# Operands of the up projection stored tile by tile in runs of 2 KB, and the 1/rms row of the attention output spread by a product with ones

## Chip, cores and metric

One Trainium2 chip, one of its cores. The metric is device time in microseconds (us) of one launch, the median over runs. Engines are called as in the profile: PE (TensorE, with PEld for its weight loads), DVE (VectorE), ACT (ScalarE), POOL (GpSimd) and SP (SyncE, which here only issues transfers).

## The reference, cut to what matters

One layer of a hybrid decoder on 2064 prompt rows (16 meta tokens and 2048) and 32 sample rows (8 sequences of 4), model width 1024, inner width 2816, all in fp32.

```python
q, k, v, u = _project(_rmsnorm(x, norm1), w_in)         # one input projection
att = _head_norm(attention(q, k, v, lam), sub_g)        # differential attention, per-head RMSNorm:
                                                        #   o * rsqrt(mean(o * o) + EPS) * g * (1 - lam_init)
ssm_out = _ssm(u, ...)                                  # state space half
x = x + concat([att, ssm_out]) @ w_out                  # output projection
xn = _rmsnorm(x, norm2)
a, c = xn @ w_gate, xn @ w_up                           # the up projection (gate and up)
x = x + (gelu(causal_conv3(a)) * c) @ w_down
```

The sample rows attend to 2048 cached keys and values each, which are gathered by a page table.

## The kernel before, in words

The 2096 rows are 17 tiles of 128 (the last has 48). Products of full accuracy are made of three products in a reduced fp32 format (`mm3`, lines 80 to 82), whose operands are split into a high and a low part by `split` (line 68 on ACT, line 69 on DVE). A scheduler with pools of buffers sets the order of the instructions on each engine when the kernel is built; code that is written later can so fill in where an earlier part waits.

**Attention and output.** `attend` works head by head, in two halves of the rows. It leaves the head outputs untouched by the norm in the DRAM scratch `OT`, and 1/rms as a row per head in the DRAM scratch `RR` (`attend_rms`, `attend_rms_store`: products SS, the chain rs_v, rs_y, rs_t on DVE and POOL, the transpose tpr, a store). `out_heads` then makes one tile of the output projection: it loads the rows of x (`oxt`), the head outputs into `ot[:, 0]`, and the 1/rms row of each head, spread over the 128 partitions by a broadcast transfer, into `ot[:, 1]` (line 1195). POOL multiplies the two (line 1196), ACT and POOL split the result into `oa` (lines 1198, 1199), and 24 products `po` follow for the two halves of the width, each added to `oxt` by DVE (line 1206). `out_norm` norms the rows (line 166 on ACT, the chain of `rsqrt`, line 171 on DVE), transposes them on PE (`tp`, line 179) and stores them as operands.

Tiles 0 to 5 are filler in the attention stage: their pool `fil` has a single PSUM bank for all their products and transposes, and single buffers. Tiles 6 to 15 come after attention, in double buffers and four PSUM banks, where the norm of a tile stands behind the products of the next. This stretch is called the tail below. Tile 16 comes much later, in the up projection.

**Sample attention.** The cached keys are gathered (`kv`, line 607 on POOL), transposed on PE (`tps`, line 632), split (`kT`) and multiplied with the queries (`Sp`, line 638). It is filler from the tail on, well into the up projection.

**Up projection.** It goes by Strassen's scheme in Winograd's form: the even and odd tiles of a block of rows are two halves, and seven operands are made of their quarters (`keep` in `out_norm`). They lie in the DRAM scratch `XB`, for each of three blocks (tiles 0 to 5, 6 to 11, 12 to 16), for each partition and operand four rows of k with up to 384 columns, 128 for each pair of tiles. `load_tokens` loads an operand in two halves of k and splits each into `xb`. `load_up` loads the weights of a unit (256 columns of gate or up) in two loads `uraw`; a unit has seven products of 12 matmuls each for each of the four k (`product`: 84 matmuls). The pool `fr` has four slots `raw` of 4 KB per partition for weights; in later blocks the first half of an operand uses them too. The other halves use slots of the pool `fz` (`z` and `A`, two each), which also hold the conv's data.

Every DMA issued on SP goes in order through one queue, so a load that waits for its buffer holds those behind it.

Of the kernel before, what the change touches and what calls it, by code (L numbers as in the profile page):

```python
# [10 lines left out]
F32 = mybir.dt.float32  # L11
# [4 lines left out]
ALU = mybir.AluOpType  # L16
# [4 lines left out]
P = 128  # L21
# [8 lines left out]
H = 4  # L30
# [16 lines left out]
BLOCKS = [(0, 6), (6, 12), (12, NT)]  # L47
# [13 lines left out]
class Step:  # L61
# [41 lines left out]
    def constants(self, cp, tp):  # L103
        nc, i = self.nc, self.i
# [3 lines left out]
        nc.vector.tensor_copy(self.identB, self.ident)  # L108
        self.half = cp.tile([P, 16], F32, name="half")
        nc.vector.memset(self.half, -0.5)  # L110
        self.ones = cp.tile([P, 32], F32, name="ones")
        nc.vector.memset(self.ones, 1.0)
        cm = tp.tile([P, P], F32, name="cm")
        nc.sync.dma_start(out=cm, in_=i["c_causal"])
# [19 lines left out]
    def scratch(self, dp):  # L134
        self.KST = dp.tile([H, 2, P, TP], F32, name="KST")
        self.QST = dp.tile([2, H, 2, 64, TP], F32, name="QST")
        self.VST = dp.tile([TP, H * P], F32, name="VST")
        self.VNS = dp.tile([NS * TS, H * P], F32, name="VNS")
        self.UT = dp.tile([512, CH, NU], F32, name="UT")
        self.XNT = dp.tile([6, P, 2, KT, 2 * P], F32, name="XNT")  # L140
        self.OT = dp.tile([H, P, T], F32, name="OT")
        self.RR = dp.tile([H, RRW], F32, name="RR")
        self.TBL = dp.tile([3, G, NST, NJ], F32, name="TBL")
        self.GT = dp.tile([CH, 512, NC], F32, name="GT")
        self.ST = dp.tile([2, 4, P, T], F32, name="ST")
        self.X1 = dp.tile([T, D], F32, name="X1")
        self.XB = dp.tile([len(BLOCKS), P, 7, 4, 3 * P], F32, name="XB")
        self.MT = dp.tile([2, P, 11, T], F32, name="MT")

    def load_x(self, xt, t):  # L150
# [1034 lines left out]
    def out_heads(self, t, wp, pp):  # L1185
        nc, gp = self.nc, self.nc.gpsimd
        n = rows_of(t)
# [3 lines left out]
        ot = wp.tile([P, 2, H, P], F32, name="ot", tag="ot")  # L1191
        nc.sync.dma_start(out=ot[:, 0, :, :n], in_=self.OT[:, :, tk].rearrange("h p t -> p h t"))

        for a, b, f in ((0, NM, 0), (NM, P, P)) if t == 0 else ((0, n, t * P + P - NM),):
            nc.sync.dma_start(out=ot[:, 1, :, a:b], in_=self.RR[:, f : f + b - a].unsqueeze(0).to_broadcast([P, H, b - a]))
        gp.tensor_tensor(out=ot[:, 0, :, :n], in0=ot[:, 0, :, :n], in1=ot[:, 1, :, :n], op=ALU.mult)
        a = wp.tile([P, 2, H, P], F32R, name="oa", tag="oa")
        nc.scalar.activation(a[:, 0, :, :n], ot[:, 0, :, :n], AF.Copy)
        gp.tensor_tensor(out=a[:, 1, :, :n], in0=ot[:, 0, :, :n], in1=a[:, 0, :, :n].bitcast(F32), op=ALU.subtract)
        for hf in range(2):  # L1200
            c = slice(512 * hf, 512 * hf + 512)
# [8 lines left out]
    def out_norm(self, t, xt, wp, pp):  # L1210
        nc, gp = self.nc, self.nc.gpsimd
        n = rows_of(t)
        xs = self.normed(wp, xt, n, self.g2)
        blk = min(t // 6, 2)
        at = (t - BLOCKS[blk][0]) // 2 * P
        last = t == NT - 1
        m = n // 2 if last else P
        if t % 2 == 0:
# [5 lines left out]
                nc.scalar.activation(x[:, b, :, :m], tp[:, :, z * m : z * m + m], AF.Copy)  # L1224

        def keep(op, x, o=1):
            nc.scalar.dma_start(out=self.XB[blk, :, op : op + o, :, at : at + m], in_=x)

        if t % 2 == 0:
            keep(0, ev[:, :, :, :m], 2)  # L1230
# [38 lines left out]
    def load_tokens(self, blk, z):  # L1269

        L = width_of(blk)
        op = self.PLACE[z]
        x = self.fx.tile([P, 2, 4, 3 * P], F32R, name="xb", tag=f"xb{op}")
        for k in (0, 2):
            if blk and k == 0:
                raw = self.fr.tile([P, 4, 256], F32, name="xraw", tag="raw", bufs=4).rearrange("p k f -> p (k f)")
            else:

                tag = "A" if blk or k else "z"
                raw = self.fz.tile([P, 6 * P + 2 * (tag == "A")], F32, name="xraw", tag=tag, bufs=2)  # L1280
            raw = raw[:, : 6 * P].rearrange("p (k c) -> p k c", k=2)
            self.nc.sync.dma_start(out=raw[:, :, :L], in_=self.XB[blk, :, op, k : k + 2, :L])
            self.split(x[:, 0, k : k + 2, :L], x[:, 1, k : k + 2, :L], raw[:, :, :L])
        self.xs[z] = x

    def load_up(self, unit):
# [470 lines left out]
```

## Time and profile before

| | |
|---|---|
| median of 3 runs | 2932.37 us (2930.18 to 2940.95) |
| the profiled execution's own time | 2934.36 us |
| its span, first to last instruction | 2932.2 us |
| mean granted PE clock | 0.974 of full speed |
| busy share of the span | PE 94%, PEld 81%, DVE 76%, ACT 48%, POOL 34% |
| transfers | 526.81 MB, mean 180 GB/s |

Busy time of PE counts the modelled ends of pipelined matmuls; idle time of PE is what is left of a stretch. A wait names the instruction that waited, its engine, and what released it. The share of a DMA queue is the time its packets took, as a part of what 16 engines have in the stretch.

### The profile page before, as it was taken

How to read it: one execution, taken by the hardware profiler on the slowest of the kernel's cores; microseconds unless marked ns; L12 is line 12 of the kernel's file. 1: busy time of each engine (PE TensorE's matmuls, PEld its weight loads, DVE VectorE, ACT ScalarE, POOL GpSimd, SP SyncE). 2: the span in 40 equal slices, each digit the busy share in tenths (PEclk: the TensorE clock that was granted, in tenths of full speed). 3: DMA queues.
4: the chain of work that ended last, by engine and by line, in shares of the span. 5: the costliest groups of instructions: out<-in, count | busy, mean ns of one | idle time of the engine just before them, and what ended most of it. 6: DMA issues, size and time to landing. Idle time of an engine off the chain costs nothing. (4 is left out here: it accounts for less than half of the span.)

```text
span 2932.2 us, 43446 instructions
## 1 busy us (share of the span) xinstructions
PE 2742.1 (94%) x14872; PEld 2360.8 (81%) x14872; DVE 2216.4 (76%) x4308; ACT 1397.6 (48%) x2850; POOL 985.0 (34%) x1383
## 2 busy tenths in 40 slices
PE   6889989989999999787999999999999999999999
PEld 6876667867888777676998899988998998777776
DVE  6738876757778888567898878888788996675565
ACT  4323223545556566335566556665555664222233
POOL 4525542114444566554333422343222442000000
PEclk9999999999999999899999999999999999999999
DMA  7975876976764432487455446464454346775562
GB/s 222 258 190 141 211 219 166 239 217 188 222 190 146 117 114 83 145 265 241 145 173 186 155 146 206 152 196 147 133 167 154 118 129 237 266 239 189 168 219 86
DMA packets 450965, 526.81 MB, mean 180 GB/s; under 512 B 91369, under 2 KB 353401, under 8 KB 449720
## 3 DMA queue, kind: packets, MB, share of 16 engines
q1 hardware_dynamic: 359000, 382.86, 44.1%
q10 hardware_dynamic: 72848, 72.79, 7.5%
q0 software_dynamic: 18896, 68.39, 7.4%
q8 instruction: 117, 1.92, 0.3%
q14 instruction: 104, 0.85, 0.1%
HBM read 387.61 MB, written 135.14 MB: 178 GB/s over the span
## 5 line engine op out<-in xcount | busy, mean ns | idle before, releaser
L80 PE MATMUL g<-xb,uw 128*128 128x384 f32 (+1 forms) x1848 | 596.3, 325 | 9.5 <-ACT uw L68 3.7
L81 PE MATMUL g<-xb,uw 128*128 128x384 f32 (+1 forms) x1848 | 595.6, 323 | 1.6 <-DVE xb L69 1.6
L82 PE MATMUL g<-xb,uw 128*128 128x384 f32 (+1 forms) x1848 | 583.6, 323 | 1.6 <-DVE uw L69 1.6
L80 PEld LDWEIGHTS g<-xb,uw 128*128 128x128 f32 x1848 | 347.6, 188 | 21.8 <-ACT uw L68 5.1
L81 PEld LDWEIGHTS g<-xb,uw 128*128 128x128 f32 x1848 | 348.4, 189 | 9.8 <-issue 2.3
L82 PEld LDWEIGHTS g<-xb,uw 128*128 128x128 f32 x1848 | 345.2, 188 | 9.0 <-DVE uw L69 3.1
L475 ACT ACTIVATE p<-S,nms 128x484 f32<-128x484 f32 (+11 forms) x360 | 209.8, 588 | 158.3 <-DVE nms L474 137.0
L69 DVE TENSOR_TENSOR uw<-uraw,uw 128x512 fp32r<-128x512 f32 x330 | 241.8, 739 | 27.0 <-ACT uw L68 25.1
L68 ACT ACTIVATE uw<-uraw 128x512 fp32r<-128x512 f32 x330 | 200.5, 625 | 115.0 <-PE g L82 72.9
L474 DVE TENSOR_REDUCE nms<-S 128x1 f32<-128x484 f32 (+11 forms) x360 | 191.3, 556 | 41.7 <-PE S L469 26.1
L80 PE MATMUL pq<-dw,da 128*128 128x512 f32 x528 | 208.3, 396 | 13.9 <-DVE dO L1586 7.6
L81 PE MATMUL pq<-dw,da 128*128 128x512 f32 x528 | 208.1, 395 | 0.0
L82 PE MATMUL pq<-dw,da 128*128 128x512 f32 x528 | 200.4, 394 | 2.3 <-DVE da L69 2.3
L95 POOL TENSOR_TENSOR rs_y<-rs_v,half 128x8 f32<-128x8 f32 (+4 forms) x77 | 105.3, 1370 | 244.8 <-DVE rs_v L90 225.5
L80 PE MATMUL pj<-wh,x 128*128 128x512 f32 (+1 forms) x408 | 169.9, 418 | 6.7 <-ACT wh L74 4.3
L81 PE MATMUL pj<-wl,x 128*128 128x512 f32 (+1 forms) x408 | 170.1, 417 | 4.8 <-DVE wl L75 4.8
L68 ACT ACTIVATE da<-dt 128x1024 fp32r<-128x1024 f32 (+1 forms) x68 | 71.0, 1045 | 215.5 <-PE pq L82 142.1
L82 PE MATMUL pj<-wh,x 128*128 128x512 f32 (+1 forms) x408 | 169.6, 416 | 0.0
L468 PE MATMUL S<-kt,qs 128*128 128x484 f32 (+11 forms) x360 | 145.5, 406 | 22.8 <-ACT p L475 14.4
L1308 POOL TENSOR_TENSOR uraw<-uraw 128x512 f32<-128x512 f32 x66 | 106.3, 1610 | 176.2 <-DVE s L1306 127.1
L507 DVE SCALAR_TENSOR_TENSOR p<-p,f 128x412 f32<-128x412 f32 (+13 forms) x164 | 139.5, 863 | 25.1 <-POOL p L505 24.9
L505 POOL TENSOR_TENSOR p<-p,g 128x412 f32<-128x412 f32 (+13 forms) x164 | 156.2, 980 | 3.4
(430 smaller groups left out, 6917.6 us busy)
## 6 DMA issues: line engine op xcount, KB each, us to landing
dt<-MT SPq DMA_DIRECT2D x99, 512.0 KB
uraw<-in_w_gate_dram SPq DMA_DIRECT2D x66, 512.0 KB
uraw<-in_w_up_dram SPq DMA_DIRECT2D x66, 512.0 KB
raw<-in_w_in_dram SPq DMA_DIRECT2D x80, 256.0 KB
MT<-z ACTq DMA_DIRECT2D x44, 384.0 KB
qs<-QST SPq DMA_DIRECT2D x128, 128.0 KB
draw<-in_w_down_dram SPq DMA_DIRECT2D x55, 256.0 KB
dT<-in_w_down_dram SPq DMA_DIRECT2D x55, 256.0 KB
```

The costliest lines, as they stand in the source:

```text
L68: nc.scalar.activation(hi, src, AF.Copy)
L69: nc.vector.tensor_tensor(out=lo, in0=src, in1=hi.bitcast(F32), op=ALU.subtract)
L80: mm(out, lhsT=lh, rhs=rh, start=start, stop=False, skip_group_check=goes_on)
L81: mm(out, lhsT=lh, rhs=rl, start=False, stop=False, skip_group_check=goes_on)
L82: mm(out, lhsT=ll, rhs=rh, start=False, stop=stop, skip_group_check=goes_on)
L95: nc.gpsimd.tensor_tensor(out=y, in0=v, in1=e, op=ALU.pow)
L468: nc.tensor.matmul(dst, lhsT=qs[:, 0, c, qa : qa + M], rhs=kt[c][:, x:y], start=True, stop=False)
L474: nc.vector.tensor_reduce(out=nms[:M, z : z + 1], in_=dst, axis=AX.X, op=ALU.max, negate=True)
L475: nc.scalar.activation(p[:M, Z + x : Z + y], dst, AF.Exp, bias=nms[:M, z : z + 1], accum_out=sms[:M, z : z + 1])
L505: nc.gpsimd.tensor_tensor(out=pw[1][:M, x], in0=pw[1][:M, x], in1=g[:M, z : z + 1].to_broadcast([M, x.stop - x.start]), op=ALU.mult)
L507: nc.vector.scalar_tensor_tensor(out=w[:M, x], in0=w[:M, x], scalar=fs[0][:M, z : z + 1], in1=pw[1][:M, x], op0=ALU.mult, op1=ALU.add)
L1308: gp.tensor_tensor(out=a21, in0=a11, in1=a21, op=ALU.subtract)
```

## The change

Two edits are made together.

The scratch `XB` gets the order block, partition, operand, pair of tiles, k, column, instead of block, partition, operand, k, column of the block. A store of one pair's operand is then one run of 4 x 128 numbers (2 KB) per partition and operand, where it was four runs of 512 B. `load_tokens` loads the first two pairs of tiles of an operand as one run of 4 KB per partition into a slot `raw` of `fr`, in every block, and the third pair (24 columns in the last block) into a slot `A` of `fz`; before, it took two halves of k, in block 0 in slots `z` and `A`. For the last tile each operand is stored by a transfer of its own.

The 1/rms row of each head is loaded into one partition alone. A product on PE of a row of ones with it (fp32, one partition deep, up to 512 columns) spreads it over the partitions in a PSUM bank `rrb`, and the multiplication with the head outputs is done by DVE out of that bank, not by POOL. The constant `ones` grows to 128 columns for it.

```diff
-        self.XB = dp.tile([len(BLOCKS), P, 7, 4, 3 * P], F32, name="XB")
+        self.XB = dp.tile([len(BLOCKS), P, 7, 3, 4, P], F32, name="XB")
...
-            nc.sync.dma_start(out=ot[:, 1, :, a:b], in_=self.RR[:, f : f + b - a].unsqueeze(0).to_broadcast([P, H, b - a]))
-        gp.tensor_tensor(out=ot[:, 0, :, :n], in0=ot[:, 0, :, :n], in1=ot[:, 1, :, :n], op=ALU.mult)
+            nc.sync.dma_start(out=ot[0:1, 1, :, a:b], in_=self.RR[:, f : f + b - a].unsqueeze(0))
+        rr = pp.tile([P, 512], F32, name="rrb", tag="ps").rearrange("p (h c) -> p h c", h=H)
+        nc.tensor.matmul(rr[:, :, :n], lhsT=self.ones[0:1, :], rhs=ot[0:1, 1, :, :n], start=True, stop=True)
+        nc.vector.tensor_tensor(out=ot[:, 0, :, :n], in0=rr[:, :, :n], in1=ot[:, 0, :, :n], op=ALU.mult)
...
-        at = (t - BLOCKS[blk][0]) // 2 * P
+        at = (t - BLOCKS[blk][0]) // 2
...
-            nc.scalar.dma_start(out=self.XB[blk, :, op : op + o, :, at : at + m], in_=x)
+
+            for z in range(o) if last else [slice(0, o)]:
+                to = self.XB[blk, :, op + z, at, :, :m] if last else self.XB[blk, :, op : op + o, at]
+                nc.scalar.dma_start(out=to, in_=x[:, z])
...
-        for k in (0, 2):
-            if blk and k == 0:
-                raw = self.fr.tile([P, 4, 256], F32, name="xraw", tag="raw", bufs=4).rearrange("p k f -> p (k f)")
-            else:
-
-                tag = "A" if blk or k else "z"
-                raw = self.fz.tile([P, 6 * P + 2 * (tag == "A")], F32, name="xraw", tag=tag, bufs=2)
-            raw = raw[:, : 6 * P].rearrange("p (k c) -> p k c", k=2)
-            self.nc.sync.dma_start(out=raw[:, :, :L], in_=self.XB[blk, :, op, k : k + 2, :L])
-            self.split(x[:, 0, k : k + 2, :L], x[:, 1, k : k + 2, :L], raw[:, :, :L])
+
+        raw = self.fr.tile([P, 4, 256], F32, name="xraw", tag="raw", bufs=4).rearrange("p (j h) (l c) -> p j (h l) c", j=2, c=P)
+        self.nc.sync.dma_start(out=raw, in_=self.XB[blk, :, op, 0:2])
+        hi, lo = [x[:, s, :, : 2 * P].rearrange("p k (j c) -> p j k c", c=P) for s in range(2)]
+        self.split(hi, lo, raw)
+
+        raw = self.fz.tile([P, 6 * P + 2], F32, name="xraw", tag="A", bufs=2)[:, : 4 * P].rearrange("p (k c) -> p k c", c=P)
+        n = L - 2 * P
+        self.nc.sync.dma_start(out=raw[:, :, :n], in_=self.XB[blk, :, op, 2, :, :n])
+        self.split(x[:, 0, :, 2 * P : L], x[:, 1, :, 2 * P : L], raw[:, :, :n])
```

The scheduler orders every engine anew from the attention stage's first filler tile on. Three places show it; line numbers past 1194 differ between the two kernels by up to five.

On PE, at the start of the tail (tpr is the transpose of the last 1/rms row, po the output products of tile 6, tps the transposes of gathered keys), the kernel before has:

```order
L552 MATMUL SS_12784<-ones_72,o2_11820 128x1 x8
L564 MATMUL tpr_12804<-ident_63,rs_y_12796 8x128
L80 MATMUL po_13903<-owh_13435,oa_13900 128x512
L81 MATMUL po_13903<-owl_13436,oa_13900 128x512
L82 MATMUL po_13903<-owh_13435,oa_13900 128x512
```

and 25 more products of this kind before the first tps. The changed kernel has there:

```order
L564 MATMUL tpr_12804<-ident_63,rs_y_12796 8x128
L1197 MATMUL rrb_13911<-ot_13908,ones_72 128x512
L632 MATMUL tps_14778<-ident_63,kv_14774 128x128 x2
L80 MATMUL po_13917<-owh_13435,oa_13914 128x512
L81 MATMUL po_13917<-owl_13436,oa_13914 128x512
L80 MATMUL po_13931<-owh_13435,oa_13914 128x512
L81 MATMUL po_13931<-owl_13436,oa_13914 128x512
L1197 MATMUL rrb_13951<-ot_13948,ones_72 128x512
L632 MATMUL tps_14778<-ident_63,kv_14776 128x128 x2
L82 MATMUL po_13917<-owh_13435,oa_13914 128x512
```

The product with ones stands ahead of each tile's output products, and these are cut up by key work. Between tpr and the first product of the up projection PE had 128 tps and 61 Sp; now it has 180 tps, 87 Sp and ten rrb, with the same 240 po and 80 tp.

On POOL, at the same place (ot is multiplied in line 1196, oa is the low part, qbd and kv belong to the gathered keys), the kernel before has:

```order
L1196 TENSOR_TENSOR ot_13896<-ot_13896 128x512
L95 TENSOR_TENSOR rs_y_12796<-rs_v_12795,half_70 128x8
L1199 TENSOR_TENSOR oa_13900<-ot_13896,oa_13900 128x512
L1196 TENSOR_TENSOR ot_13934<-ot_13934 128x512
L618 MEMSET qbd_14731 128x1088
L607 DMA kv_14742<-in_cache_k_dram,idx_14699 128x1024
...
L1199 TENSOR_TENSOR oa_13938<-ot_13934,oa_13938 128x512
L624 COPY qbd_14731<-qhl_14727 64x4x4 x8
L1196 TENSOR_TENSOR ot_14000<-ot_14000 128x512
```

and the changed kernel:

```order
L95 TENSOR_TENSOR rs_y_12796<-rs_v_12795,half_70 128x8
L618 MEMSET qbd_14763 128x1088
L607 DMA kv_14774<-in_cache_k_dram,idx_14731 128x1024
...
L624 COPY qbd_14763<-qhl_14759 64x4x4 x8
L1201 TENSOR_TENSOR oa_13914<-ot_13908,oa_13914 128x512
L1201 TENSOR_TENSOR oa_13954<-ot_13948,oa_13954 128x512
L95 TENSOR_TENSOR rs_y_13990<-rs_v_13989,half_70 128x1
```

The multiplications of tiles 6, 7 and 8 are gone from POOL, and the copies into qbd, which wait for gathered keys, stand ahead of the first low parts.

On SP, at the start of the up projection (oxt is the tail's last load of x), the kernel before has:

```order
L1190 DMA oxt<-X_104 128x1024 x3
L1293 DMA uraw<-in_w_gate_dram 128x4x256 x2
L1293 DMA uraw<-in_w_up_dram 128x4x256 x2
L1282 DMA xraw<-XB 128x768 x5
L1293 DMA uraw<-in_w_gate_dram 128x4x256 x2
L1282 DMA xraw<-XB 128x768 x5
L1293 DMA uraw<-in_w_up_dram 128x4x256 x2
```

and the changed kernel:

```order
L1190 DMA oxt<-X_104 128x1024
L1298 DMA uraw<-in_w_gate_dram 128x4x256 x2
L1281 DMA xraw<-XB 128x1024 x2
L1287 DMA xraw<-XB 128x512 x2
L1281 DMA xraw<-XB 128x1024 x2
L1287 DMA xraw<-XB 128x512 x2
L1281 DMA xraw<-XB 128x1024 x3
L1298 DMA uraw<-in_w_up_dram 128x4x256
L1287 DMA xraw<-XB 128x512
L1298 DMA uraw<-in_w_up_dram 128x4x256
```

The second unit's weights (the first two loads from w_up) stood ahead of ten token loads and now stand behind eleven and twelve.

## Rows read from the trace of the kernel before

**Rows 1.** By stretch: length, busy PE, PEld, DVE, ACT, POOL, clock, DMA share, GB/s.
```profile
960.00:1216.00 256.00, 232.37 (x1238) 188.10 (x1236) 214.39 (x516) 153.03 (x446) 155.74 (x244) 0.97 0.35 102
...
1224.00:1342.00 118.00, 94.98 (x447) 78.49 (x446) 65.03 (x105) 38.37 (x71) 63.12 (x65) 0.89 0.83 258
1342.00:1362.00 20.00, 14.60 (x66) 11.04 (x65) 11.22 (x16) 10.36 (x18) 9.22 (x9) 0.80 0.71 212
...
1400.00:2500.00 1100.00, 1084.63 (x6533) 1010.98 (x6533) 933.92 (x1526) 631.67 (x1097) 351.76 (x408) 1.00 0.51 165
```

**Rows 2.** Waits of PE from 1216 to 1362 us: total, times, longest.
```profile
PE tp L179 <- DVE xs L171: 16.7, 5, 5.0
PE tps L632 <- DMA kv<-in_cache_k_dram,idx: 10.3, 5, 4.3
PE tpr L564 <- DVE rs_y L99: 5.9, 1, 5.9
```

**Rows 3.** ACT's DMA queue from 1048 to 1062 us: packets, MB, share of 16 engines.
```profile
q10 hardware_dynamic: 2624, 1.31, 33.1%
```

**Rows 4.** The same queue from 2300 to 2440 us.
```profile
q10 hardware_dynamic: 2016, 4.01, 7.6%
```

**Rows 5.** DMA queues and issues from 1224 to 1362 us (q0 carries the gathers).
```profile
q10 hardware_dynamic: 19760, 14.42, 32.8%
...
q0 software_dynamic: 2446, 8.91, 19.1%
...
ot<-RR SPq DMA_DIRECT2D x8, 256.0 KB
...
kv<-in_cache_k_dram,idx POOLq DMA_INDIRECT x18, 6.8
```

**Rows 6.** PE in order of time: start, duration, line, operation, count.
```profile
305.23 0.61 PE L1041 MATMUL yp<-U,Tz 128*128 128x266 f32 x2
305.68 0.61 PE L1042 MATMUL yp<-Hh,Cs 128*128 128x266 f32 x2
```

**Rows 7.** Groups by line, whole span: count, busy us, mean ns, idle before.
```profile
L1206 DVE TENSOR_TENSOR oxt<-po,oxt 128x512 f32<-128x512 f32 (+1 forms) x34 | 23.3, 684 | 17.7 <-PE po L82 16.9 <-DMA oxt<-X 0.7
L1196 POOL TENSOR_TENSOR ot<-ot 128x512 f32<-128x512 f32 (+1 forms) x17 | 23.1, 1359 | 33.4 <-DMA ot<-RR 27.3 <-ACT sl L641 3.3 <-DVE rs_y L99 2.7
```

**Rows 8.** Longest wait of PE from 950 to 1216 us.
```profile
PE S L468 <- ACT p L475: 11.1, 11, 2.7
```

**Rows 9.** A wait of POOL from 950 to 1216 us.
```profile
POOL ot L1196 <- DMA ot<-RR: 12.2, 4, 7.9
```

**Rows 10.** DVE in order of time at the last 1/rms row.
```profile
1219.95 1.22 DVE L96 TENSOR_TENSOR rs_t<-rs_y 128x8 f32<-128x8 f32 x1 [1.76 <-POOL rs_y L95]
...
1223.37 0.17 DVE L99 TENSOR_TENSOR rs_y<-rs_y,rs_t 128x8 f32<-128x8 f32 x1
```

**Rows 11.** A wait of POOL from 1216 to 1362 us.
```profile
POOL qbd L624 <- DMA kv<-in_cache_k_dram,idx: 5.9, 1, 5.9
```

**Rows 12.** PE in order of time: key work in the tail.
```profile
1274.87 1.53 PE L638 MATMUL Sp<-kT,qbd 128*128 128x512 f32 x6
1276.24 0.81 PE L632 MATMUL tps<-ident,kv 128*128 128x128 f32 x6
```

**Rows 13.** SP's queue in order of time: token loads of block 0.
```profile
1215.55 3.10 SPq L1282 DMA_DIRECT2D xraw<-XB  x3
...
1356.87 12.29 SPq L1282 DMA_DIRECT2D xraw<-XB  x5
...
1373.38 8.52 SPq L1282 DMA_DIRECT2D xraw<-XB  x5
```

**Rows 14.** By stretch, as rows 1: the two changes of block.
```profile
1800.00:1860.00 60.00, 55.94 (x325) 51.59 (x324) 52.87 (x78) 35.69 (x63) 17.10 (x16) 1.00 0.63 210
2200.00:2260.00 60.00, 53.90 (x380) 51.37 (x379) 53.70 (x103) 34.30 (x66) 14.89 (x26) 0.97 0.48 149
```

**Rows 15.** Groups by line from 1224 to 1342 us, as rows 7.
```profile
L96 DVE TENSOR_TENSOR rs_t<-rs_y 128x1 f32<-128x1 f32 x10 | 15.9, 1592 | 9.7 <-POOL rs_y L95 9.6
```

More of the change, by code (lines that the diff above doesn't have):

```diff
@@ L110, in constants @@
         nc.vector.memset(self.half, -0.5)
-        self.ones = cp.tile([P, 32], F32, name="ones")
+        self.ones = cp.tile([P, P], F32, name="ones")
         nc.vector.memset(self.ones, 1.0)
```

## Prediction

> **What bounds the kernel now.** I read the stretches first: busy time of each engine in stretches from 960 us on [rows 1]. The reader is to see that TensorE is nearly full in most of them. The up projection (1400 to 2500 us) has 1084.6 of 1100 us busy, 15 us idle; nothing that is moved within it can win more. The attention stage with its six filler tiles (960 to 1216 us) leaves 23.6 us idle. The stretch that is different is the tail, from the last row of 1/rms to the first up product (1224 to 1362 us): 109.6 of 138 us busy, so 28.4 us idle, at a granted clock of 0.89 and 0.80, where the transfer engines are at 0.83 and 0.71. There ten output tiles run with the cached keys as filler. Then the waits: TensorE waits there for the normed rows of the tile before (16.7 us), for gathered keys (10.3 us), and once 5.9 us for the last 1/rms [rows 2]. Last the transfer queues, because both edits act on them.
>
> **The stores of the operands.** Before, each store of a tile goes in runs of 512 B. In a stretch where the ACT queue stored nothing else [rows 3], 2624 packets took 33.1% of 16 engines over 14 us: 74.1 us, 28.3 ns each. In one where it stored the conv product, mean 1990 B, a packet took 0.076 x 16 x 140 / 2016 = 84.4 ns [rows 4], so 87 ns for 2 KB against 4 x 28.3 = 113 ns. A pair of tiles stores 7 x 128 = 896 runs of 2 KB; 896 x 26 ns over 16 engines is 1.5 us, and five pairs in the tail 7.3 us of all engines. The Trainium skill (DMA: Bandwidth & Descriptors, section Specifications) gives 512 B as the size from which a transfer runs at line rate. By that rule these stores would not get cheaper; the rows differ, 18 against 24 GB/s for one engine, and I go by the rows.
>
> **The row of 1/rms.** The broadcast wrote 128 x 4 runs of 512 B; at 28.3 ns that is 0.9 us of all engines, and eight of them are issued in the tail [rows 5], 7.2 us. What is left is four runs. Together the transfers lose 14.5 us of about 112 (0.83 x 118 + 0.71 x 20).
>
> The product with ones is new. Its price is from the only long product of this type without the reduced format: 266 columns in two passes, from one start to the next 0.45 us [rows 6]; 512 columns are 0.87 us. Sixteen tiles and a short one are 14.2 us of TensorE: 5.2 in the filler tiles, 8.7 in the tail, 0.3 later. The multiplication leaves POOL (1359 ns, 17 times) and comes to VectorE, where a tile of that size out of PSUM takes 684 ns [rows 7]. The chain of a tile is about as long as before: 0.87 + 0.68 against 1.36 us.
>
> In the filler stage I take +5 us: TensorE is 91% busy and what it waits for is softmax work [rows 8], on which VectorE gains 6 x 0.68 and POOL loses 6 x 1.36 us. The floor is 0 (the idle 23.6 us take the products); the ceiling adds the 12.2 us that POOL waited for this transfer [rows 9], which TensorE, with everything queued behind the product, could now wait instead: +17.
>
> At 1216 to 1224 us POOL did the multiplication of tile 6 and 7 while TensorE waited, and VectorE's small steps of that chain took 1.2 us beside it, the last one, behind it, 0.17 [rows 10]. Now the first output product waits behind 0.87 + 0.68 us and ScalarE's split, some 2 us, but those steps run without POOL beside them; three at 0.3 instead of 1.2 give the 2.7 back. I take 0, from -2.7 to +2.
>
> **The tail.** The order rows show the multiplications gone from POOL, so the one of tile 8 no longer stands behind the copies that waited 5.9 us for keys [rows 11], and the output products are cut up by key work. Up to the first up product there are now 180 transposes of keys instead of 128 and 87 score products instead of 61. A product takes 0.23 us from start to start and a transpose at most 0.81 / 6 = 0.135 us [rows 12], so this is some 12 us of work taken out of the up projection into a stretch that has idle time. The price is 6.5 more gathers there; a gather costs 0.191 x 16 x 138 / 17 over 16 engines, 1.55 us [rows 5], so 10 us of the 14.5 are given back. TensorE then has 109.6 + 8.7 + 12 = 130 of 138 us, less with fewer slow clocks. I let the stretch grow by 4 us: -8. Without any relief it is +8.7 + 2, +11; if nearly all of the 28.4 us of idle and half of what the slow clock costs (96.2 us of full clock in 109.6: 13.4) went, less the products, it is 28.4 + 6.7 - 8.7, about -26.
>
> **Start of the up projection.** Token loads and weights now share the four slots of one tile. Of the fourteen loads of the first unit's tokens three were made at 1215 us and one soon after, ten from 1356.9 on [rows 13]; now two small ones stand early, two large ones behind the first weights, and ten follow. New is that the second unit's weights come behind them. Its cover is the first unit's seven products, 84 matmuls of 1084.6 / 6533 = 0.166 us [rows 1], 14 us. I take +1; -1 to +8.5, the length of the second row of loads.
>
> **Block changes.** TensorE is idle 4.1 and 6.1 us there [rows 14]; the number of loads and of elements to split stays the same, in pieces of two thirds and one third instead of two halves. I take -1, from -5 to +4. Runs of 96 B remain for the last 24 columns.
>
> Sum: 5 + 0 - 8 + 1 - 1 = -3 us on the profiled execution of 2934.4 us, whose span is 2.2 us shorter; it lies 2.0 above the median, so **2929 us** as a median. Half a per cent, 14.7 us, is about what a measurement can tell from no change.
>
> **Rivals.** *Faster*: the tail is bound by transfers, not TensorE. For: 0.83 busy, key gathers late 10.3 us. Then the 14.5 us come off it whole, with half of the slow clock (7 us) and a third of what VectorE's first short step is held there, ten times 1.59 us [rows 15] against 0.17 (5 us), less the 5 of the filler: -21, 2911 us. Against: the order spends the room on more gathers.
>
> *Slower*: the product stands at the head of TensorE's queue before its row has landed. POOL waited 27.3 us for these rows, 8 times [rows 7]; POOL could afford it. If TensorE takes that over, with 5.2 of products, less the 8 us of the tail: +24, 2956 us. It decides when the waits exceed some 18 us. Against: a transfer of four runs lands earlier than one of 512.
>
> *The stores do nothing*: in the tail their packets lie beside those of two other queues, so that fewer of them may save no time. Then the relief is 7.2 us, 3 less than the extra gathers need, the stretch grows by 4 us more, and the time is 2933 us. Against it stands the difference between 28.3 and 84.4 ns. This is what the rule of the Trainium skill (DMA: Bandwidth & Descriptors, Specifications) would give.
>
> **How the numbers follow.** Forecast 0.38, faster rival 0.32, slower rival 0.18, stores that do nothing 0.12. Faster by over 0.5% 0.32, within 0.50, slower 0.18. The range, 2902 to 2956, runs from -30 (the tail's -26, -5 at the block changes, -3 before the tail, -1 at the start, +5 in the filler) to the slower rival; the forecast's own band is 2917 to 2943.
>
> **What would show it.** Right: ten products of about 0.87 us in the tail, POOL without multiplications, the ACT queue's packets there down from 19760 to some 6300, the first up product near 1365 us with more key work before it, idle TensorE in the tail under 20 us. Wrong: TensorE waiting for the row's transfer or VectorE for the tile's; a gap before the second unit; the tail shorter with the same idle share, which would mean that transfers had set it.

## The result and the profile after

The changed kernel is slower by 0.8%: 2956.39 us median of four executions (2955.33 to 2966.20) against 2931.27 us for the kernel before, ratio 1.008, 95% interval 1.0057 to 1.0104. The forecast was 2929 us, from 2902 to 2956. The time lies 0.4 us above the upper end of the range, which the slower rival had set, but that rival's mechanism is not what happened. The profiled execution took 2966.2 us, 10 us more than the median; of its 32 us over the profile before, some 25 are typical.

Both programs are cut at the same four events: the last output product of the recurrent part, the last 1/rms transposition `tpr`, the first up product, the first down product. The columns are those of [rows 1]. Before:

```profile
927.20:1223.70 296.50, 264.39 (x1419) 214.74 (x1418) 246.40 (x581) 177.46 (x510) 176.98 (x276) 0.97 0.38 112
1223.70:1361.80 138.10, 109.68 (x510) 89.66 (x511) 76.05 (x120) 48.53 (x88) 72.44 (x74) 0.88 0.81 250
1361.80:2454.70 1092.90, 1075.08 (x6535) 1006.21 (x6534) 955.39 (x1560) 647.05 (x1126) 374.28 (x431) 1.00 0.49 159
2454.70:2932.20 477.50, 454.94 (x1939) 361.93 (x1937) 283.53 (x344) 139.16 (x185) 0.95 (x3) 0.99 0.62 206
```

And after:

```profile
927.60:1215.50 287.90, 266.39 (x1430) 215.96 (x1429) 246.63 (x587) 176.04 (x508) 160.89 (x267) 0.98 0.33 105
1215.50:1391.00 175.50, 142.58 (x609) 102.84 (x609) 85.92 (x144) 58.86 (x106) 72.27 (x84) 0.86 0.61 203
1391.00:2483.20 1092.20, 1068.31 (x6458) 1001.18 (x6459) 944.45 (x1548) 638.47 (x1110) 364.29 (x412) 0.99 0.50 157
2483.20:2964.40 481.20, 455.52 (x1939) 361.84 (x1937) 283.44 (x346) 139.22 (x185) 1.12 (x3) 0.98 0.62 205
```

The attention stage is 8.6 us shorter, the tail 37.4 us longer, the up projection the same although 77 fewer TensorE instructions stand in it. In the tail TensorE is busy 32.9 us more and idle 32.9 instead of 28.4 us, at a clock of 0.86, while the transfer engines fell from 0.81 to 0.61. The waits of TensorE there, as in [rows 2]:

```profile
PE tps L632 <- DMA kv<-in_cache_k_dram,idx: 17.7, 9, 3.0
PE tp L179 <- DVE xs L171: 6.4, 3, 3.4
PE tpr L564 <- DVE rs_y L99: 3.5, 1, 3.5
PE Sp L638 <- POOL qbd L624: 2.9, 1, 2.9
```

No wait of TensorE for a row of 1/rms stands in this list, so the loss is not where the slower rival put it. The transfer queues of that stretch, as in [rows 5]:

```profile
q0 software_dynamic: 3354, 12.23, 22.5%
q10 hardware_dynamic: 6320, 14.42, 21.4%
...
kv<-in_cache_k_dram,idx POOLq DMA_INDIRECT x25, 5.5
```

The ACT queue moves the same 14.42 MB in 6320 packets (forecast 6300). It took 0.328 x 138 = 45.3 us of all engines before and 0.214 x 175.5 = 37.6 us now: the forecast relief of 7.3 us is there (7.7), and it brought nothing.

One tile of the tail, all engines in order of time (start, duration, engine, line, operation, idle before):

```profile
1253.69 1.29 POOL L1239 TENSOR_TENSOR xt<-xod,xev 128x512 f32<-128x512 f32 x1 [8.69 <-ACT xod L1226]
...
1254.49 1.12 PE L1197 MATMUL rrb<-ot,ones 1*128 1x512 f32 x2
...
1255.65 0.69 DVE L1198 TENSOR_TENSOR ot<-rrb,ot 128x512 f32<-128x512 f32 x1 [2.38 <-PE rrb L1197]
...
1257.01 0.62 ACT L1200 ACTIVATE oa<-ot 128x512 fp32r<-128x512 f32 x1
...
1257.68 0.51 PE L80 MATMUL po<-owh,oa 128*128 128x512 f32 x1
1257.73 0.99 POOL L607 DMA_INDIRECT kv<-in_cache_k_dram,idx  x1 [0.16 <-issue]
...
1261.76 1.25 POOL L1201 TENSOR_TENSOR oa<-ot,oa 128x512 fp32r<-128x512 f32 x1
...
1262.86 0.69 PE L632 MATMUL tps<-ident,kv 128*128 128x128 f32 x2 [2.96 <-DMA kv<-in_cache_k_dram,idx]
...
1268.56 0.48 PE L82 MATMUL po<-owh,oa 128*128 128x512 f32 x1
```

The product, VectorE's multiplication, ScalarE's and GpSimd's halves of the operand and the output products follow one another. From the product to the first output product that needs GpSimd's half pass 14 us, filled with key work whose gathers GpSimd issues late, behind its own waits. The product takes 1.05 us from start to start of the next at full clock (2.0 at half clock; three of the ten stood there), not 0.87.

### The profile page after: what moved, and what is told of

It reads as the page before. It is cut to its first block, busy times and chain, and to the rows that moved or that the text cites. A ratio compares the mean times of both kernels' runs of the same rounds, so it can differ in the third digit from the quotient of the medians.

```text
span 2964.4 us, 43506 instructions
## 1 busy us (share of the span) xinstructions
PE 2774.1 (94%) x14906; PEld 2374.2 (80%) x14906; DVE 2216.4 (75%) x4325; ACT 1399.0 (47%) x2850; POOL 956.6 (32%) x1366
## 5 line engine op out<-in xcount | busy, mean ns | idle before, releaser
L1313 POOL TENSOR_TENSOR uraw<-uraw 128x512 f32<-128x512 f32 x66 | 113.4, 1718 | 185.7 <-DVE s L1311 138.8
L537 PE MATMUL O<-wT,vt 128*128 128x256 f32 x576 | 144.3, 387 | 5.1 <-DVE wT L534 2.9
```

The source lines that it names most:

```text
L537: nc.tensor.matmul(O[:, :N], lhsT=v, rhs=tw[:, m - a, :N], start=(m == 0), stop=(m == nb))
L1313: gp.tensor_tensor(out=a21, in0=a11, in1=a21, op=ALU.subtract)
```

## The experiments

Ratios are to the kernel before on the same chip; "tail" and the other stretches are cut as above. Edits are against the kernel before unless another is named.

**The parts.** `both_again` is the changed kernel itself. `xb_alone` is the half of the diff on `XB` and `load_tokens`, `rr_alone` the half on `out_heads` and `ones`. `xb_fill` is `xb_alone` and `rr_fill` the kernel before, each with product and VectorE's multiplication for the first six tiles only:

```diff
+        one = t < 6
...
+            if one:
+                nc.sync.dma_start(out=ot[0:1, 1, :, a:b], in_=row)
+            else:
+                nc.sync.dma_start(out=ot[:, 1, :, a:b], in_=row.to_broadcast([P, H, b - a]))
```

> The changed kernel as it is, once more beside the kernel before on this chip, for a second profile and as a scale for the three kernels that run with it. Both theories: 1.008 of the kernel before, some 2956 us; the stretch from the last 1/rms row to the first up product near 170 us and the up projection to the down projection about as long as before (1092 us). If the profiled run stays near its median, the up projection is 5 to 10 us shorter than in the first profile.

> The new layout of the token scratch with its loads alone; the broadcast transfer and GpSimd's multiplication stay as before. Theory A (the product with ones costs the time, in the tail): not slower than before, 2920 to 2932 us; stretch from the last 1/rms row to the first up product 128 to 140 us, with the 130 transposes of keys and 64 score products that the order has there (before 128 and 61). Rival B (the token loads that share the slots of the weights start the up projection late): slower, 2945 us or more, with TensorE idle by 10 us or more in the first 100 us of the up projection.

> The product with ones and VectorE's multiplication alone; the scratch and its loads as before. Theory A: nearly the whole loss or more of it, 2955 to 2970 us: ten products of about 1.05 us in the tail, 176 transposes and 83 score products of keys there instead of 128 and 61 (some 12 us), slow clocks, and an up projection that does not get shorter by what was moved. The stage with the filler ends some 8 us earlier, as in the changed kernel. Rival B: near 2932 us.

> The new scratch with its loads, the product with ones for the six output tiles in the attention stage only, and the broadcast transfer with GpSimd's multiplication for the other eleven. Theory A: the attention stage keeps the 8 us that it gained, the tail has before's key work (130 transposes, 64 score products): 2913 to 2926 us, faster than before and than the new scratch alone. Rival C (the 8 us of the attention stage are not the product's doing, or are given back in the tail): the time of the new scratch alone within 4 us.

> The kernel before, with the product with ones only for the six output tiles in the attention stage; scratch, loads and the other eleven tiles as before. If the parts add up (attention stage about 10 us shorter, 39 us more in the tail and 12 less in the up projection for products in the tail, 14 us for the new scratch): some 10 us faster than before, ratio 0.9965, with a tail of 138 us and an up projection of 1093 us. Rival: the gain of the attention stage belongs to the run of that chip, ratio 1.000.

Measured:

| | ratio | interval | attention stage | tail | up projection | rest |
|---|---|---|---|---|---|---|
| before | 1 | | 296.5 | 138.1 | 1092.9 | 477.5 |
| both_again | 1.0106 | 1.0074 to 1.0138 | 286.2 | 178.1 | 1093.8 | 479.6 |
| xb_alone | 1.0070 | 1.0043 to 1.0096 | 296.4 | 142.5 | 1102.6 | 477.4 |
| rr_alone | 1.0082 | 1.0054 to 1.0111 | 288.0 | 177.7 | 1080.8 | 477.5 |
| xb_fill | 1.0013 | 0.9992 to 1.0035 | 290.7 | 142.8 | 1103.0 | 478.2 |
| rr_fill | 0.9961 | 0.9944 to 0.9979 | 288.9 | 136.3 | 1090.7 | 477.1 |

The times are those of one profiled execution each. Stretch by stretch the parts add up to within some 4 us of `both_again`; the ratios of the medians add up to 1.5% instead, above the 0.8 and 1.1% of the two measurements of the whole, which stays open. The product with ones gains 8 us in the attention stage, costs some 40 in the tail and gives 12 back in the up projection, where the moved key work is missing. The new scratch costs 4 in the tail and 10 in the up projection. Neither theory of the first set had this whole: A expected `xb_alone` not to be slower, B expected `rr_alone` to be neutral; `xb_fill`, expected faster than before, took the same time. `rr_fill`, which keeps only the gain, is faster than both kernels.

**Why the tail grows.** `gate_bcast` and `gate_ones` (the latter on `rr_alone`) hold the key work in the tail at the same 32 transposes and 13 score products:

```diff
+        if t == 15:
+            nc.vector.tensor_scalar(out=self.gate, in0=xs[:, 0:1], scalar1=0.0, scalar2=None, op0=ALU.mult)
...
+            nc.vector.tensor_tensor(out=idx[:, r], in0=idx[:, r], in1=self.gate.to_broadcast([P, NS]), op=ALU.add)
```

> The kernel before, with the indices of the cached keys' gathers made to depend on the normed rows of output tile 15 (a zero is added), so that the order has only the last 32 transposes and 13 score products of keys in the tail, behind the output tiles. It is the pair of the next one. Expected: TensorE idle for 40 us or more in the tail, which is then bound by the chain of a tile; tail 125 to 140 us; the up projection longer by what moved into it, some 24 us.

> As the one ahead of it, with the product with ones and VectorE's multiplication in all tiles; the amount of key work in the tail is the same, 32 transposes and 13 score products. Theory K (the loss in the tail is the key work that the scheduler added there, with its late gathers): tail at most 11 us longer than its pair's (the products themselves, 10 x 1.05). Theory C (the product in TensorE's queue makes each tile's chain longer): tail 25 us or more longer than its pair's, TensorE idle rising by more than 10 us. The attention stage is some 8 us shorter in both theories.

The tail of `gate_bcast` (ratio 1.0019, 1.0003 to 1.0035):

```profile
1218.80:1338.10 119.30, 85.03 (x367) 67.61 (x368) 54.82 (x111) 34.48 (x61) 59.65 (x61) 0.83 0.79 244
```

Its tail is a little shorter than expected (125 to 140 us), its idle time 34.3 instead of 40 us or more. That of `gate_ones` (1.0085, 1.0064 to 1.0106):

```profile
1206.60:1352.10 145.50, 111.21 (x387) 77.00 (x388) 64.27 (x120) 35.62 (x63) 48.94 (x53) 0.76 0.57 184
```

With equal key work the tail grows by 26.2 us, so theory K falls. Theory C has the size right and the place half wrong: TensorE's idle time is 34.3 us in both, and its busy time grows, by an estimate from 85.03 x 0.83 = 70.6 to 111.21 x 0.76 = 84.5 us of full clock (14, of which the products are 10.5) and by 12 us more for the slow clock. What TensorE waits for changes. In `gate_bcast` it is mostly the normed rows:

```profile
PE tp L180 <- DVE xs L172: 24.5, 8, 8.0
```

In `gate_ones` it is mostly the two halves of the operand, behind the product:

```profile
PE po L80 <- ACT oa L1202: 13.4, 9, 1.8
...
PE po L82 <- POOL oa L1203: 5.8, 5, 1.5
```

One tile of `gate_ones`, TensorE in order of time:

```profile
1227.23 1.09 PE L180 MATMUL tp<-ident,xs 128*128 128x128 f32 x8 [0.48 <-DVE xs L172]
1228.25 1.12 PE L1199 MATMUL rrb<-ot,ones 1*128 1x512 f32 x2
1231.16 0.50 PE L80 MATMUL po<-owh,oa 128*128 128x512 f32 x1 [1.79 <-ACT oa L1202]
...
1232.71 0.79 PE L82 MATMUL po<-owh,oa 128*128 128x512 f32 x1 [0.35 <-POOL oa L1203]
1233.30 0.63 PE L80 MATMUL po<-owh,oa 128*128 128x512 f32 x1
```

Nothing stands between the product and what needs its result, so TensorE waits 1.8 us, and some 5 us behind the start of the product the output products take 0.63 instead of 0.40 us. Such a wait, of 1.4 to 1.8 us, stands in nine of the ten tiles, and each of the ten has output products at half clock. In the changed kernel the scheduler has filled that gap with key work, so waits for gathers stand where this one does; without the 12 us of added key work its tail is 25 us longer, as much as here. The next two kernels and one more ask whether the product or its place is to blame. In `gate_ones_r` the row and the ones are fp32r; in `gate_k128` the row goes to 128 partitions and `lhsT` has ones in its first row and zeros below; in `early`, on `rr_alone`, the order of the code is changed:

```diff
-            xt = self.out_heads(t, wp, pp)
+            cur, a = a, self.out_operands(tiles[z + 1], wp, pp) if z + 1 < len(tiles) else None
+            xt = self.out_products(t, cur, wp, pp)
```

`out_operands` loads the head outputs and the row, and makes product, multiplication and split; `out_products` loads `oxt` and does the rest of `out_heads`.

> As gate_ones, but the row and the ones are taken in the reduced fp32 format, so that the product is one pass instead of two slow ones; the row is rounded by it, which the output shows in its last digits. Theory P (the length of the ten products counts): at full clock a product of 512 columns takes 0.23 us from start to start against 1.05, so the tail is 8 us shorter than gate_ones' 145.5 us or somewhat more, 133 to 138 us. Theory W (the wait behind the product counts, 2.5 us from the product's end to the first output product while VectorE, ScalarE and GpSimd make the operand, and the half clock that follows it): at most 8 us shorter, TensorE idle as before (34 us) or more, granted clock in the tail still under 0.8, tail 137 us or more.

> As gate_ones, but the product runs over 128 rows instead of one: the transfer writes the row to all 128 partitions, as before the change, and the stationary operand has ones in its first row and zeros in the others, so that the result is the same. Theory R (the clock falls in each tile because the product has one row): granted clock of the tail back from 0.76 to 0.83 or more, tail some 10 us shorter than 145.5 us. Theory W (it falls because of the wait behind the product, whatever its rows): clock 0.74 to 0.78, tail within 4 us of 145.5 us.

> The kernel before with the product with ones in all tiles, as rr_alone, but in the tail the operand of the next tile (its loads, product, multiplication and split) is written ahead of the output products of the tile at hand, so that these lie between the product and what needs it. The order has 116 transposes and 55 score products of keys in the tail. Theory W (the wait behind the product and the half clock that follows): the tail loses most of its 39 us: 145 us or less with 10.5 us of products in it, ratio to before 0.995 to 0.999. Theory P (the products' own length and the transfers): tail 160 us or more, ratio 1.005.

`gate_ones_r` (1.0064, 1.0043 to 1.0086) has a tail of 144.3 us, 1.2 us shorter: a product of half the time, and the wait behind it grows to some 2.0 us. The length of the product is not the cause. The tail of `gate_k128` (1.0089, 1.0063 to 1.0114):

```profile
1199.00:1339.60 140.60, 100.25 (x387) 71.64 (x388) 64.31 (x120) 35.40 (x63) 48.93 (x53) 0.84 0.67 203
```

With 128 rows the clock is back at 0.84, as theory R said, and theory W, which expected 0.74 to 0.78 behind the same waits (1.6 to 2.0 us), is wrong on the clock. But only 5 of the 11 us of busy time come off the tail, half of what R expected; the rest turns into idle time (40.3 us). This execution lies 15 us below its kernel's median (2938.55 against 2953.21 us), and by the medians 128 rows gain nothing over one (1.0089 against 1.0085). So the one row has a part in the slow clock, but the chain of a tile sets the tail, and the slow clock had filled its gaps. `early` (0.9951, 0.9931 to 0.9971) takes the chain off TensorE's path, and its tail is

```profile
1211.80:1333.20 121.40, 111.00 (x512) 83.16 (x512) 71.54 (x125) 46.71 (x86) 60.70 (x60) 0.94 0.80 253
```

Ten products are in it, the idle time is 10.4 us and the clock 0.94. TensorE in order of time there:

```profile
1243.74 1.12 PE L1189 MATMUL rrb<-ot,ones 1*128 1x512 f32 x2
1244.79 0.50 PE L80 MATMUL po<-owh,oa 128*128 128x512 f32 x1
```

The output products of the preceding tile start 1.05 us behind the product's start, without a wait. This is 17 us less tail than before the change, some 3 of them, at the prediction's prices, because 12 transposes and 6 score products fewer stand in it; and it is 24 us less than in `gate_ones`, with far more key work (116 transposes against 32). Theory P falls, and theory W holds for the wait behind the product; that the wait alone makes the slow clock is not shown (`gate_k128`). The Trainium skill (TensorE: Matmul & The Clock Gate, section HAM oscillation — how this bites in real kernels) tells of a loop whose waits for transfers throw TensorE back to the slow clock in every pass, and advises to restructure such a loop so that it stays at the fast one. The two tails, 0.76 and 0.94, go the same way, though the waits here are for ScalarE and GpSimd; `gate_k128`, with the same waits as `gate_ones` and 0.84, shows that the waits alone are not all of it.

To see whether the order alone does this, `early_bcast` is `early` with the broadcast transfer and VectorE's multiplication out of SBUF.

> As early, but with the row spread by the broadcast transfer and the multiplication by VectorE out of SBUF: no product. Theory O (only the place in the order counts): the tail is some 10 us shorter than early's 121.4 us by the products that are gone, or the same where transfers set it; ratio to before 0.991 to 0.996. Theory E (the product has a part in the gain, since the small transfers leave the queues free): tail 128 us or more, ratio 0.997 or more.

Ratio 0.9984 (0.9970 to 0.9999), tail 135.3 us. The order alone gives little; the product has a part. TensorE's first waits in `early_bcast`:

```profile
PE tp L179 <- DVE xs L171: 16.8, 5, 4.2
PE tps L632 <- DMA kv<-in_cache_k_dram,idx: 8.5, 4, 4.7
```

In `early` they are 2.5 and 5.1 us. VectorE waits for the broadcast row in `early_bcast`:

```profile
DVE ot L1188 <- DMA ot<-RR: 8.3, 4, 4.9
```

That this is what makes the normed rows late is likely, but not shown: product and small transfer always come together in `early`, and no run takes them apart. Once its chain is hidden, the edit shortens the tail.

**Why the attention stage gains.** `dve_fill` moves only GpSimd's multiplication:

```diff
-        gp.tensor_tensor(out=ot[:, 0, :, :n], in0=ot[:, 0, :, :n], in1=ot[:, 1, :, :n], op=ALU.mult)
+        eng = nc.vector if t < 6 else gp
+        eng.tensor_tensor(out=ot[:, 0, :, :n], in0=ot[:, 0, :, :n], in1=ot[:, 1, :, :n], op=ALU.mult)
```

> The kernel before with the multiplication of the six output tiles of the attention stage on VectorE instead of GpSimd; transfers stay broadcast, no product. Theory V (the attention stage gains because GpSimd loses six multiplications): from the last product of the recurrent part to the last 1/rms row 288 us as in the kernels with products there, instead of 296.5; ratio 0.997. Theory T (it gains because the row's transfer is small and the chain behind it short): 294 us or more, ratio 0.999 to 1.001.

Ratio 0.9970 (0.9951 to 0.9989), stage 288.4 us: theory V. A wait of VectorE in that stage, before the change:

```profile
DVE p L507 <- POOL p L505: 16.9, 11, 3.9
```

In the changed kernel:

```profile
DVE p L507 <- POOL p L505: 2.5, 6, 0.9
```

And in `dve_fill`, where the row still comes by broadcast:

```profile
DVE p L507 <- POOL p L505: 2.4, 4, 1.6
```

GpSimd stood 12.2 us at the multiplication waiting for rows [rows 9] and was busy with it for 1.36 us a tile, with softmax work (line 505) queued behind it, for which VectorE waited. TensorE's largest wait of the stage, 11.1 us in total before [rows 8], is in the changed kernel

```profile
PE S L468 <- ACT p L475: 4.1, 8, 1.1
```

`dve_fill` takes both the waiting and the multiplications off GpSimd; no run tells which of the two counts for more.

**Why the new scratch costs.** Four kernels have the new stores and differ in the token loads alone: in the first block slots shared with the weights (`raw`) or of their own (`z` and `A`), and operands cut by columns, as in the change, or by halves of k, in three transfers each. The first unit is measured from its first up product's matmul to the 85th, with which the second unit begins. `xb_own` keeps the cut by columns:

```diff
+        for j in () if blk else range(2):
+            raw = self.fz.tile([P, 6 * P + 2 * j], F32, name="xraw", tag="zA"[j], bufs=2)[:, : 4 * P].rearrange("p (k c) -> p k c", c=P)
+            self.nc.sync.dma_start(out=raw, in_=self.XB[blk, :, op, j])
```

`xb_halves` has the halves of k and the slots of before; `xb_halves_raw` is that with `if k == 0` for `if blk and k == 0`:

```diff
+            for j in range(2):
+                self.nc.sync.dma_start(out=raw[:, :, j * P : j * P + P], in_=self.XB[blk, :, op, j, k : k + 2])
+            self.nc.sync.dma_start(out=raw[:, :, 2 * P : L], in_=self.XB[blk, :, op, 2, k : k + 2, :n])
```

> The new scratch and its stores, but token loads by halves of k as before, into the slots of before (z and A in the first block), each half now of three transfers instead of one, in runs of 1 KB; broadcast transfer as before. Theory L (the loads cost the time: they share the four slots of the weights in the first block): the first unit of the up projection takes 24 us as before instead of 32, up projection near 1093 us instead of 1103, ratio 1.001 to 1.003. Theory S (the stores cost it, or smaller things spread over the tail): up projection 1100 us or more or a tail of 142 us or more, ratio 1.005 or more.

> As xb_alone, but in the first block of the up projection the first two pieces of a token operand are loaded one by one into the slots z and A instead of a slot that the weights use; the later blocks load as in xb_alone. Theory L (the shared slots hold back the second unit's weights): their loads are issued some 30 us ahead of the first up product again, the first unit takes 24 us instead of 32, ratio to before 0.999 to 1.002. Theory S (what else the new scratch changes): ratio 1.005 or more as in xb_alone, or a first unit of 30 us.

> As xb_halves (operands loaded by halves of k, each half in three transfers), but in the first block the first half goes into a slot that the weights use and the second into the slot A, as the pieces of the changed kernel do. Theory L (the shared slots cost it): first unit 30 us or more, ratio 1.005 or more, as xb_alone. Theory K (the cut by columns costs it, because every product needs all pieces of its operand at its first matmul, while of an operand cut by k the first half is enough for the first six): first unit 25 us or less, ratio 1.000 to 1.003, as xb_halves. Both together: between.

| slots, cut | ratio | interval | first unit, us |
|---|---|---|---|
| before | 1 | | 23.7 |
| own, k (xb_halves) | 1.0009 | 0.9996 to 1.0023 | 23.3 |
| own, columns (xb_own) | 1.0048 | 1.0029 to 1.0066 | 32.9 |
| shared, k (xb_halves_raw) | 1.0078 | 1.0060 to 1.0096 | 33.5 |
| shared, columns (xb_alone) | 1.0070 | 1.0043 to 1.0096 | 31.9 |

The slow first unit is idle time and slow clock. The first 24.2 us of the up projection before, and the first 32.8 us of it in `xb_alone`:

```profile
1361.80:1386.00 24.20, 21.75 (x122) 18.99 (x121) 24.16 (x34) 18.89 (x32) 16.93 (x17) 1.00 0.76 258
```

```profile
1360.20:1393.00 32.80, 26.86 (x136) 24.72 (x137) 27.89 (x36) 20.36 (x32) 15.44 (x18) 0.84 0.73 249
```

The tail, which ends with the first up product, took 136.3 and 139.6 us with slots of their own and 143.0 and 142.5 us with shared ones (order of the table). The up projection as a whole does not follow the first unit: `xb_halves` took 1105.5 us for it in its profile, not the 1093 that theory L expected but more than the 1100 of theory S. That execution lies 8 us above its kernel's median, and its matmuls of the last block come 0.134 us after one another on average, against 0.130 before, some 8 us in all (the last section shows the same in `xb_fill`). The ratio, from twelve executions, is on the side of theory L.

Of the two kernels cut by k, which differ in slots alone, the shared one loses 0.7%. SP's queue in `xb_halves`, whose first up product is at 1352.1 us:

```profile
1318.63 5.29 SPq L1299 DMA_DIRECT2D uraw<-in_w_gate_dram  x2
1324.22 1.81 SPq L1299 DMA_DIRECT2D uraw<-in_w_up_dram  x2
```

In `xb_halves_raw`, first up product at 1365.5 us:

```profile
1326.50 5.41 SPq L1299 DMA_DIRECT2D uraw<-in_w_gate_dram  x2
...
1379.34 1.19 SPq L1299 DMA_DIRECT2D uraw<-in_w_up_dram  x2
```

The second unit's weights are issued 28 us ahead of the first product in the one and 14 us behind it in the other. But slots of their own do not mend the cut by columns: in `xb_own` these weights go out 30 us ahead, and the first unit is slow all the same, with this wait of TensorE in it:

```profile
PE g L80 <- ACT xb L68: 4.4, 1, 4.4
```

What of it is the cut and what the 21 loads through four slots stays open. Two kernels join the parts again: `early_own` is `early` with the new scratch and the loads of `xb_own`, `early_halves` with those of `xb_halves`.

> The whole change with both mendings: new scratch with the first block's tokens in slots of their own, product with ones in all tiles, the next tile's operand ahead of the output products. If these two causes explain the loss, and the new stores give nothing: the time of early within 0.2%, ratio to before 0.993 to 0.998. If a loss is left that neither explains: 1.000 or more.

> As early, with the new scratch and its stores, and token loads by halves of k in the slots of before. If the stores give or cost nothing: ratio 0.994 to 0.998, the time of early or up to 0.2% more. If the longer runs of the stores free the queues in the tail: under 0.994. If the new scratch costs something apart from the cut and the slots: 0.999 or more.

They took 1.0014 (0.9996 to 1.0031) and 0.9996 (0.9980 to 1.0011), with tails of 127.9 and 122.3 us and up projections of 1106.6 and 1112.3 us; `early` has 121.4 and 1093.5. No form of the new scratch paid: both lie 0.4 to 0.6% above `early`, where they were expected beside it, and the loss stands in the up projection. In `early_own` most of it is the first unit, 37.9 us against 27.0 in `early`, as in `xb_own`. In `early_halves` it is not: its first unit takes 30.4 us, and beyond it some 15 us are lost, of which slower matmuls in the last block make some 5. The rest is not explained. `early`, without the new scratch, has the lowest ratio, but `rr_fill` (0.9961) lies within its interval: with a tail 15 us shorter, `early` has an attention stage, an up projection and a rest that are each 2 to 4 us longer in the profiles.

## Why the prediction was wrong

Working back through its terms, on the profiled executions:

- **Stores and row transfers**: right in size (7.7 us for the stores against 7.3, packets 6320 against 6300), and right that the packets of 512 B cost more than a quarter of one of 2 KB. But the busy transfer engines were not what the tail waited for, and the freed share ended nothing earlier; beside `early`, too, the new stores gave nothing (tail 122.3 us in `early_halves` against 121.4). What helped there was the product with its small row transfer (against `early_bcast`).
- **Filler stage, +5, and the last 1/rms row, 0**: measured -8.6 together. The failed step is "POOL could afford it". The wait of 12.2 us at the multiplication was counted as a cost that TensorE might take over, not as one that GpSimd, together with 1.36 us for each multiplication, handed to the softmax work behind it in its queue. In the changed kernel TensorE did not take it over.
- **The tail, -8**: the step that failed, with the most weight. "TensorE then has 109.6 + 8.7 + 12 = 130 of 138 us" treated the idle 28.4 us as room. It was the gaps of a chain, and the change put TensorE itself into that chain: `gate_ones` shows +26 us with no key work added (by the estimate above 10.5 of products, 3.5 of other full-clock work, 12 of slow clock). The 12 us of moved key work were counted rightly, and `rr_alone` gives 12.1 back in the up projection; but they lengthened the tail by as much, so the move brought nothing. The tails of `rr_alone` and `gate_ones` bear this out: 32.2 us between them, for 144 transposes and 70 score products, at most 36 us at the prediction's prices. Net +25 instead of -8. The step "The chain of a tile is about as long as before" compared its instructions one by one and left out that on GpSimd the multiplication could start when its data landed, while the product had to stand in TensorE's order.
- **The product's price**, 0.87: measured 1.05 at full clock and 2.0 at half clock. A small error, since `gate_ones_r` gains only 1.2 us from a shorter one.
- **Start of the up projection, +1, and block changes, -1**: measured about +11 after the moved key work is allowed for (+10 in `xb_alone`). The bound of 8.5 us was the right size for the first unit (+8), but "Its cover is the first unit's seven products, 14 us" was taken as enough. The 14 us are the mean of the whole up projection; this unit took 23.7 us even before, and now the weights went out behind the token loads, 12 to 16 us into the unit.
- **The rest**, not forecast: +3.7 and +2.1 in the two profiles of the changed kernel, -0.4 to +0.7 in the four part kernels. Over all profiles this stretch took 474.5 (`gate_k128`) to 481.3 us (`early`), so nothing of it can be put down to the change.

Of the rivals, *Slower* had the time, by luck, and the wrong place; *Faster* was not seen; *The stores do nothing* was right about their worth, by another reason than the one given. What would have shown the tail's loss: asking, for the instruction put on TensorE, what stands in its order between it and the first instruction that needs its result. The order rows show only key work there.

## What to carry to other kernels

Work moved onto the engine that is the bound becomes a link of a chain there: its length matters less than what stands behind it in that engine's order while the other engines finish, so write the next tile's operand ahead of this tile's products (2911 us instead of 2950 for the same product). Idle time inside a dependent chain is no room for more filler; filler moved there lengthened this stretch by about what it takes, and its price was only returned later. Work and waits on an engine with spare time still cost when other engines' inputs are queued behind them, and a load that waits for a shared slot delays every load behind it in its queue.

## What the runs showed of the hardware

The one-row product took 1.12 us for its two passes and a product of 128 rows over the same columns 1.02 us, so few rows save nothing; and with the one-row product the granted clock of the same tail was 0.76 instead of 0.84. Over the whole kernel it was 0.968 to 0.970 in the five runs with one row and 0.972 to 0.973 in the five with 128, without a gain in the median time. Executions also differ where nothing waits: in the last block of the up projection TensorE was busy without a gap in `xb_fill`,

```profile
2322.30:2385.30 63.00, 63.00 (x475) 63.00 (x474) 58.22 (x130) 37.06 (x73) 22.16 (x35) 1.00 0.39 121
```

0.133 us for a matmul at a granted clock of 1.00, where the profile before has, in the same place,

```profile
2321.80:2381.80 60.00, 59.87 (x468) 59.63 (x468) 57.98 (x127) 36.22 (x71) 22.67 (x32) 1.00 0.40 126
```

0.128 us. Over the 1848 matmuls of that block this comes to some 8 to 9 us. The start of the program, too, up to the first transposition of a 1/rms row, where both do the same work, took 726.8 us in the profile of `early_bcast` and 737.0 us in that of the changed kernel. This is part of why single profiles lie up to 15 us off the medians; what sets it is open.
